# A hybrid decoder trunk on one core: window copies, side work, keys and values of layer B, planner durations, state rows, recurrent weights and tile sizes changed together

## The chip, the cores and the metric

The kernel runs on one core of one Trainium2 chip. The metric is the device time of one execution in microseconds; the median of several runs is compared. TensorE is called PE, VectorE DVE, ScalarE ACT, GpSimd POOL and SyncE SP, as in the profile.

## The reference

Four layers in a row, A, B, C and A again, for a prompt of 1024 tokens and 8 sequences of 4 sample tokens that share the weights; model width 1024, all float32. After each layer stands a LayerNorm of `ALPHA * x + mixer(x)`.

```python
def short_conv_mixer(x, buf, w_in, conv_w, w_out):            # layer A, twice
    h, b_gate, c_gate, z = jnp.split(x @ w_in, 4, axis=-1)
    conv, new_buf = causal_dwconv(c_gate * h, buf, conv_w)
    return (jax.nn.silu(z) * b_gate * conv) @ w_out, new_buf

def nsa_mixer(x, past_rows, win_buf, w_in, w_cmp, w_out):     # layer B
    proj = x @ w_in                                           # q, six kinds of k and v, gates, z
    full = jnp.concatenate([past_rows, rows], axis=1)
    kv_c = jnp.einsum('bnjcgd,cjgd->bncgd', blocks, w_cmp)    # 32 rows into one
    # attention over compressed blocks, 16 selected blocks and a window of 512
    y = (o * jax.nn.silu(z)) @ w_out
    all_win = jnp.concatenate([win_buf, win_new], axis=1)
    return y, rows, all_win[:, all_win.shape[1] - keep:]

def rglru_mixer(x, h0, buf, w_in, conv_w, conv_b, w_a, b_a, w_x, b_x, lam, w_out):   # layer C
    u, z = jnp.split(x @ w_in, 2, axis=-1)
    uc, new_buf = causal_dwconv(u, buf, conv_w)
    r, i = sigmoid(block_dense(uc, w_a) + b_a), sigmoid(block_dense(uc, w_x) + b_x)
    a = jnp.exp(-RG_C * softplus(-lam) * r)
    h = scan(a, sqrt(1 - a * a) * i * uc)                     # h[t] = a[t] h[t-1] + b[t]
    return (jax.nn.silu(z) * h) @ w_out, h[:, -1], new_buf
```

Besides the activations the outputs hold the new states: the last rows ahead of each convolution, the last `h`, the new rows of keys and values, and for the 8 sample sequences the window cache `nsa_win_sample`. Its 512 rows of 256 numbers are the old rows 4 to 511, moved up by four, and four new rows. The 508 old rows of a sequence are 520,192 bytes that are only copied.

## The kernel before

All 1056 tokens go together, in three token pieces j of 352 columns, and in 8 chunks c of 128 channels. Activations lie with the channels on the partitions. Every float32 operand is split into a high and a low part, so that the product of one chunk and one piece with a 1024-wide weight is 24 matmuls of 128x128 by 128x352: 8 chunks of the contraction, three products each.

Instructions are not issued at once but recorded (`Rec`, line 241; therefore nearly all rows of the profile name the helper's line L310). At the end of a `part()` the planner `Rec.lay` (line 378) simulates the recorded steps with assumed durations and so fixes the order of PE, ACT, DVE and POOL; for a DMA from SP it assumes 100 ns of issue and 360 bytes per ns on a shared bus. The order of SP's DMAs comes from a scheduler behind it. Tiles come from rings: `w` (3 weight blocks, split), `ws` (4 or 5 staging tiles), `big` (18 tiles of 2112 columns), `c` (8 or 9 tiles of 512 columns), and in PSUM 5 banks `mm` and 3 banks `aux`. A tile can only be written when its last reader is through.

Three parts are recorded, with the attention over the prompt, ordered by a table of its own (`Plan`), between the second and the third:

- The first: the load of x, `layer_a(0)` (line 947), `out_phase` 0 (line 685) with its norm, and the projection of layer B (`b_project`, line 1375). Beside layer A0 goes `compress` (line 1271), which gathers 64 batches of 1 MB of the paged cache by indirect DMA from POOL, writes half of each on as raw rows (`raw<-big`) and reduces the other half on DVE and POOL. `share` (line 610) lets it go on by RATE = 0.7 batches with each of the 96 products of layer A0. At its end the sums go out to `kcd`.
- The second: `decode` (line 1622), the attention of the sample tokens: scores in 36 units, and the selection of blocks (`decode_select`) at units SELT = (3, 9, 18), which reads `sel<-kcd`.
- The third: `out_phase` 1 behind layer B, `layer_c` (line 1078), `out_phase` 2, `layer_a(1)`, called A1 here, and `final_phase` (line 814).

`out_phase` takes the pairs (c, j) in order: a dense product over all eight U (outputs of the mixer), added to x, the sums for the norm; `d = y - k` goes to a scratch tensor `dd` in DRAM, and the norm of a piece j reads it back (`c<-dd`), normalises it and splits it into the x tiles that the next layer's matmuls read. `put_rows` (line 935) transposes the state rows SC, which each chunk of a layer fills, with eight PE transposes (`aux<-idf,SC`) and writes them out; layers A and C end with it. In layer B the products for keys and values (`mm<-x,w` or `mm<-big,x`, 128x384) are taken for nine row tiles in groups of four, copied by ACT to tiles `c`, and `put_k` writes the keys, with the low half of one group to a scratch tensor `kl`. Layer C loads each weight when its chunk comes (`load_w`, `weights`). Layer C also issues the eight copies of the old window rows, DRAM to DRAM; they wait for nothing that holds them, and SP's order has them in the first part, beside layer A0.

Of the kernel before, what the change touches and what calls it, by code (L numbers as in the profile page):

```python
# [18 lines left out]
P = 128  # L19
# [221 lines left out]
class Rec:  # L241
# [136 lines left out]
    def lay(self):  # L378
# [45 lines left out]
        while True:  # L424
# [23 lines left out]
            if e == "SP":  # L448
                free[e] = s + 100
                bus = max(bus, s + 100) + o.size / 360  # L450
                o.end = bus + 2000
            else:
                free[e] = o.end = s + cost
                if o.size:
                    bus = max(bus, o.end) + o.size / 360
                    o.end = bus + 2000
# [42 lines left out]
class Trunk:  # L499
    def __init__(self, ctx, tc, io):  # L500
        self.ctx, self.tc, self.nc, self.io = ctx, tc, tc.nc, io
        self.rec = Rec(tc)
# [31 lines left out]
    def work(self, stack, nws, ncc):  # L534

        self.nwork = getattr(self, "nwork", 0) + 1
        self.nws = nws
# [22 lines left out]
    def ct(self, w=512, dt=F32):  # L560
        return self.cc.tile([P, 512], dt, name="c")[:, 0:w]
# [123 lines left out]
    def out_phase(self, pm, wsrc, U, X, ln, lp, res=None, done={}, spill=None, final=None, nxt=()):  # L685
# [81 lines left out]
        for c, j in order:  # L767
            if c not in W:
                take(c)
# [44 lines left out]
    def final_phase(self, pm, wsrc, U, X, ln, lp):  # L814
# [77 lines left out]
        def squares(j, n, c0, c1):  # L892
# [4 lines left out]
            for i in range(3):  # L897
                x = half(j, c0 // 4, i)[:, c0 % 4 * P:(c1 - 1) % 4 * P + P]
                nc.scalar.activation(self.ct((c1 - c0) * P), x, AF.Square, bias=nk[:, i:i + 1], accum_out=sq[:, j, i, n:n + 1])

        running = []
        for c, j in [(c, j) for c in range(4) for j in range(3)] + [(c, j) for j in range(3) for c in range(4, NCH)]:
            if c not in W:
                take(c)
# [42 lines left out]
    def layer_a(self, pm, a, X, lp, side=None, nxt=()):  # L947
# [3 lines left out]
        U = [None] * NCH  # L951
        SC = lp.tile([P, NCH, 36 if self.later else 18], F32, name="SC")
# [14 lines left out]
        for c in range(NCH):  # L967
# [6 lines left out]
            def step(w, j):  # L974
# [19 lines left out]
                else:  # L994
# [11 lines left out]
                    for a0, b0, v in parts:  # L1006
# [4 lines left out]
                        self.split(uh, ul, v, "act", "dve")  # L1011
            U[c] = self.view2(self.big(F32R))
# [10 lines left out]
        self.put_rows(pm, SC, 18, [(0, 2, io["o_conv_a_prompt"][a, 0]), (2, 18, io["o_conv_a_sample"][a].rearrange("b t f -> (b t) f"))])  # L1023
# [54 lines left out]
    def layer_c(self, pm, X, lp):  # L1078
# [7 lines left out]
        def conv_in(c, js):  # L1086

            if c not in UC:
                W = self.get_w(("c", c), lambda: self.load_w(win[:, c * P:(c + 1) * P], ("c", c)))
# [42 lines left out]
        def gates(c):  # L1132
            n, i = c // 2, c % 2
            if i == 0:
                WA[n] = weights(n)
# [47 lines left out]
        def gate_out(c):  # L1183
            h2, i = H[c // 2], c % 2
            W = self.load_w(win[:, D + c * P:D + (c + 1) * P], ("z", c))
            u = self.view2(self.big(F32R))
            U[c] = u
            for j in range(3):
# [7 lines left out]
                self.split(u[:, 0, sl], u[:, 1, sl], th, "act", "pool")  # L1196

            nc.sync.dma_start(win_s[c, 0:508, :], cache[c, 4:512, :], rk=[("z", c)])
        UC, GT, WA, H = {}, {}, {}, {}
        win_s = io["o_nsa_win_sample"][0].rearrange("b t c g d -> b t (c g d)")  # L1200
        cache = io["cache_nsa_win"][0].rearrange("b t c g d -> b t (c g d)")
# [1221 lines left out]
```

## Time and profile before

| what | value |
|---|---|
| median of three runs | 2428.99 us (2427.99 to 2431.45) |
| the profiled execution | 2425.75 us, span 2423.7 us |
| busy: PE, DVE, ACT, POOL | 2305.6, 1583.6, 1203.7, 959.3 us |
| granted clock, mean | 0.977 |

The stages, in us from the span's start: load of x to 35; layer A0 to 414, `out_phase` 0 from 430 to 534, norm and layer B's first keys and values to 600, the rest of the projection to 690, decode to 880, the prompt's attention to about 1475, `out_phase` 1 and its norm to 1600, layer C to 1832, `out_phase` 2 to 1926, layer A1 to 2302, `final_phase` to the end; the last matmul ends at 2407.85.

How the views are read. The windows table gives for a stretch (start:end) its length, then the busy time of PE, PE's weight loads, DVE, ACT and POOL with the number of instructions of each, the granted clock of PE (1.00 is 2.4 GHz, 0.50 is 1.2 GHz), the mean busy share of the 16 DMA engines, and the GB/s that they moved. A row of a timeline begins with start and length; the bracket at its end holds the time for which the engine had been idle and what released it. In the chain of waits each piece is what the next one waited for. PE does 24 matmuls of 128x352 in 3.9 to 4.0 us where nothing holds it up.

### The profile page before, as it was taken

What the parts mean: (1) busy time and instruction counts of PE and PEld (TensorE: products, weight loads), DVE (VectorE), ACT (ScalarE), POOL (GpSimd) and SP (SyncE); (2) the same over time, 40 slices, a digit from 0 to 9 for tenths busy, and PEclk for the clock granted to TensorE, in tenths of its full rate; (3) what the DMA queues carried; (4) which work ended last, traced back from release to release, by engine and by line L of the source; (5) the groups of instructions that cost most, each with busy time, mean ns of one, the idle gap of its engine ahead of it and who ended that gap; (6) DMA issues with size and microseconds to landing.
All of it is one profiled execution on the core that took longest, in us unless ns stands there. A gap on an engine that the chain in (4) does not pass through costs nothing. (4 is left out here: it accounts for less than half of the span.)

```text
span 2423.7 us, 41400 instructions
## 1 busy us (share of the span) xinstructions
PE 2305.6 (95%) x14801; PEld 2234.8 (92%) x14801; DVE 1583.6 (65%) x3686; ACT 1203.7 (50%) x2757; POOL 959.3 (40%) x1070
## 2 busy tenths in 40 slices
PE   8999997997989989999999999989999999999996
PEld 8999997996888879999999989989999999999996
DVE  5786875575358877777777777787765753433336
ACT  3211111234438878888888883487863442222233
POOL 3454543213137765565555552333463320000131
PEclk9999999997999999999999999999999999999998
DMA  7999988347356752111111234331113321111112
GB/s 260 351 350 338 321 291 281 98 151 245 104 175 230 247 201 56 33 47 43 47 48 41 78 123 124 117 103 53 53 47 118 99 67 53 44 44 53 35 46 72
DMA packets 334642, 320.34 MB, mean 132 GB/s; under 512 B 19462, under 2 KB 301542, under 8 KB 324964
## 3 DMA queue, kind: packets, MB, share of 16 engines
q1 hardware_dynamic: 325220, 250.58, 33.4%
q0 software_dynamic: 9216, 67.11, 7.4%
q8 instruction: 117, 1.92, 0.3%
q14 instruction: 89, 0.73, 0.1%
HBM read 237.31 MB, written 84.48 MB: 133 GB/s over the span
## 5 line engine op out<-in xcount | busy, mean ns | idle before, releaser
L310 PE MATMUL mm<-x,w 128*128 128x352 f32 x5760 | 948.9, 326 | 29.6 <-DVE ws L310 10.3
L310 PEld LDWEIGHTS mm<-x,w 128*128 128x128 f32 x5760 | 936.4, 190 | 36.6 <-DVE w L310 7.6
L310 PE MATMUL mm<-big,w 128*128 128x352 f32 x2208 | 375.4, 325 | 1.0 <-ACT c L310 1.0
L310 PEld LDWEIGHTS mm<-big,w 128*128 128x128 f32 x2208 | 357.2, 189 | 2.8 <-ACT c L310 1.3
L310 POOL TENSOR_TENSOR w<-ws,w 128x1024 fp32r<-128x1024 f32 (+1 forms) x43 | 104.8, 2438 | 445.8 <-ACT w L310 426.7
L1968 DVE TENSOR_TENSOR c<-T,c 128x512 fp32r<-128x512 f32 (+1 forms) x320 | 204.7, 648 | 49.3 <-ACT c L1964 44.9
L1964 ACT CAST c<-T 128x512 fp32r<-128x512 f32 (+1 forms) x320 | 174.3, 551 | 59.3 <-PE T L1960 37.7
L310 ACT CAST w<-ws 128x1024 fp32r<-128x1024 f32 (+2 forms) x116 | 120.3, 1038 | 163.3 <-PE mm L310 119.4
L641 PE MATMUL D<-x,w 128*128 128x352 f32 x1008 | 195.5, 330 | 2.2 <-DVE big L2095 2.2
L1870 PE MATMUL A<-big 128*128 128x320 f32 (+11 forms) x832 | 181.5, 334 | 3.4 <-DVE ast L1895 1.6
L1975 PE MATMUL O<-c,big 128*128 128x256 f32 x1056 | 180.4, 291 | 0.5 <-ACT c L1964 0.2
L310 POOL TENSOR_TENSOR big<-big,ws 128x1024 f32<-128x1024 f32 (+1 forms) x38 | 89.6, 2358 | 199.0 <-DMA big<-in_cache_nsa_kv,idx 103.9
L641 PEld LDWEIGHTS D<-x,w 128*128 128x128 f32 x1008 | 159.8, 188 | 5.7 <-DVE big L2095 3.5
L310 DVE TENSOR_TENSOR big<-big 128x256 f32<-128x256 f32 (+3 forms) x204 | 150.5, 758 | 21.7 <-POOL big L310 20.3
L310 DVE TENSOR_TENSOR w<-ws,w 128x1024 fp32r<-128x1024 f32 (+2 forms) x73 | 93.9, 1286 | 105.6 <-ACT w L310 104.8
L310 ACT CAST big<-aux 128x352 fp32r<-128x352 f32 (+3 forms) x116 | 45.4, 399 | 229.9 <-DVE aux L310 160.6
L1975 PEld LDWEIGHTS O<-c,big 128*128 128x128 f32 x1056 | 147.2, 189 | 2.5 <-DVE c L1968 0.7
L1928 POOL TENSOR_SCALAR pr<-pr,G,ast 128x32 f32<-128x32 f32 (+6 forms) x192 | 125.6, 668 | 47.1 <-DVE ast L1939 41.3
L1870 PEld LDWEIGHTS A<-big 128*128 128x128 f32 x832 | 134.3, 193 | 10.0 <-PE A L1870 2.2
L310 ACT ACTIVATE aux<-ws,PT 128x352 f32<-128x352 f32 (+2 forms) x72 | 42.7, 593 | 172.5 <-DVE ws L310 167.9
L1924 ACT ACTIVATE pr<-pr,ast 128x32 f32<-128x32 f32 (+6 forms) x192 | 118.4, 619 | 18.3 <-DVE ast L1895 17.4
L310 DVE SCALAR_TENSOR_TENSOR c<-c,mm 128x352 f32<-128x352 f32 x125 | 64.1, 515 | 92.3 <-ACT c L310 54.6
(286 smaller groups left out, 4032.7 us busy)
## 6 DMA issues: line engine op xcount, KB each, us to landing
ws<-in_a_w_in SPq DMA_DIRECT2D x64, 512.0 KB
raw<-big SPq DMA_DIRECT2D x128, 256.0 KB
big<-raw SPq DMA_DIRECT2D x128, 256.0 KB
c<-dd SPq DMA_DIRECT2D x48, 176.0 KB
xs<-x SPq DMA_DIRECT2D x24, 352.0 KB
x<-xs SPq DMA_DIRECT2D x8, 1056.0 KB
ws<-in_a_w_out SPq DMA_DIRECT2D x16, 512.0 KB
ws<-in_c_w_in SPq DMA_DIRECT2D x16, 512.0 KB
```

What stands on the lines that cost most here:

```text
L310: getattr(real, name)(*[f(x) for x in a], **{q: f(x) for q, x in k.items()})
L641: self.nc.tensor.matmul(ps, a, b, start=n == 0, stop=n == 23 and last)
L1870: nc.tensor.matmul(o, q[:, hl, i * P:(i + 1) * P], k, start=m == 0, stop=m == 1)
L1924: nc.scalar.activation(S[:, a:a + m], S[:, a:a + m], AF.Exp, bias=st[:, k:k + 1], scale=-1.0, accum_out=st[:, 3 + k:4 + k])
L1928: nc.gpsimd.tensor_scalar(S[:, a:a + m], S[:, a:a + m], G[:, i, 16 * k + h:16 * k + h + 1], st[:, 6 + k:7 + k], op0=ALU.mult, op1=ALU.mult)
L1964: nc.scalar.copy(x["H"][:, 0:n], x["tp"][:, 0:n])
L1968: nc.vector.tensor_sub(x["L"][:, 0:n], x["tp"][:, 0:n], x["H"][:, 0:n].bitcast(F32))
L1975: nc.tensor.matmul(O, v, M[:, y * P:(y + 2) * P], start=done[0] == 0, stop=done[0] == total - 1)
```

## The change

- **Window copies.** The eight DRAM-to-DRAM copies of layer C are gone. In layer A1 (the call without side work) chunk c = 0 to 3 takes a `big` tile and loads two sequences into it, each as 127 partitions of four rows (127x1024); chunk c + 1 writes them out.
- **Side work.** RATE goes from 0.7 to 0.75.
- **Planner.** A DMA from SP is now assumed to take 400 ns of issue, the bus 330 bytes per ns.
- **State rows.** Layers A and C no longer call `put_rows` at their end but leave the call in `self.rows`; `out_phase` and `final_phase` make it ahead of the pair (2, 0).
- **Layer B.** `put_k` takes the second group first; the keys and values of four row tiles share one `big` tile, `four`, in place of four `c` tiles.
- **Selection.** SELT becomes (5, 10, 18).
- **Layer C's weights.** `take` and `fetch` load a block one ahead of its use in ORDER_C.
- **Small tiles.** In the third part the ring `c` has 12 tiles of 384 columns, not 9 of 512; the squares of `final_phase` are written to an `aux` bank in PSUM.

```diff
@@ -448,4 +448,4 @@
             if e == "SP":
-                free[e] = s + 100
-                bus = max(bus, s + 100) + o.size / 360
+                free[e] = s + 400
+                bus = max(bus, s + 400) + o.size / 330
                 o.end = bus + 2000
@@ -454,3 +454,3 @@
                 if o.size:
-                    bus = max(bus, o.end) + o.size / 360
+                    bus = max(bus, o.end) + o.size / 330
                     o.end = bus + 2000
@@ -501,3 +501,3 @@
         self.ctx, self.tc, self.nc, self.io = ctx, tc, tc.nc, io
-        self.rec = Rec(tc)
+        self.rec, self.rows = Rec(tc), None
 
@@ -533,6 +533,6 @@
 
-    def work(self, stack, nws, ncc):
+    def work(self, stack, nws, ncc, cw=512):
 
         self.nwork = getattr(self, "nwork", 0) + 1
-        self.nws = nws
+        self.nws, self.cw = nws, cw
         self.ws = Ring(self.rec, self.pool(f"ws{self.nwork}", nws, stack), "ws", nws) if nws else None
@@ -559,4 +559,4 @@
 
-    def ct(self, w=512, dt=F32):
-        return self.cc.tile([P, 512], dt, name="c")[:, 0:w]
+    def ct(self, w, dt=F32):
+        return self.cc.tile([P, self.cw], dt, name="c")[:, 0:w]
 
@@ -767,2 +767,5 @@
         for c, j in order:
+            if (c, j) == (2, 0) and self.rows:
+                self.rows()
+                self.rows = None
             if c not in W:
@@ -898,3 +901,3 @@
                 x = half(j, c0 // 4, i)[:, c0 % 4 * P:(c1 - 1) % 4 * P + P]
-                nc.scalar.activation(self.ct((c1 - c0) * P), x, AF.Square, bias=nk[:, i:i + 1], accum_out=sq[:, j, i, n:n + 1])
+                nc.scalar.activation(self.aux(pm)[:, 0:(c1 - c0) * P], x, AF.Square, bias=nk[:, i:i + 1], accum_out=sq[:, j, i, n:n + 1])
 
@@ -902,2 +905,4 @@
         for c, j in [(c, j) for c in range(4) for j in range(3)] + [(c, j) for j in range(3) for c in range(4, NCH)]:
+            if (c, j) == (2, 0):
+                self.rows()
             if c not in W:
@@ -951,2 +956,3 @@
         U = [None] * NCH
+        win_s, win_c = (io[x][0].rearrange("b t c g d -> b t (c g d)") for x in ("o_nsa_win_sample", "cache_nsa_win"))
         SC = lp.tile([P, NCH, 36 if self.later else 18], F32, name="SC")
@@ -1011,2 +1017,11 @@
                         self.split(uh, ul, v, "act", "dve")
+            if side is None and c < 5:
+
+                if c:
+                    for i in range(2):
+                        nc.sync.dma_start(win_s[2 * c - 2 + i, 0:508, :].rearrange("(p t) f -> p t f", t=4), keep[:, i])
+                if c < 4:
+                    keep = self.big()[0:127, 0:2048].rearrange("p (b t f) -> p b t f", b=2, t=4)
+                    for i in range(2):
+                        nc.sync.dma_start(keep[:, i], win_c[2 * c + i, 4:512, :].rearrange("(p t) f -> p t f", t=4))
             U[c] = self.view2(self.big(F32R))
@@ -1022,3 +1037,4 @@
             pass
-        self.put_rows(pm, SC, 18, [(0, 2, io["o_conv_a_prompt"][a, 0]), (2, 18, io["o_conv_a_sample"][a].rearrange("b t f -> (b t) f"))])
+        self.rows = lambda: self.put_rows(pm, SC, 18, [(0, 2, io["o_conv_a_prompt"][a, 0]),
+                                                       (2, 18, io["o_conv_a_sample"][a].rearrange("b t f -> (b t) f"))])
         return U
@@ -1088,3 +1104,3 @@
             if c not in UC:
-                W = self.get_w(("c", c), lambda: self.load_w(win[:, c * P:(c + 1) * P], ("c", c)))
+                W = take(("c", c))
                 g = self.wsl(1083)
@@ -1134,3 +1150,3 @@
             if i == 0:
-                WA[n] = weights(n)
+                WA[n] = take(("g", n))
                 H[n] = self.big()[:, 0:2 * T].rearrange("p (a n) -> p a n", a=2)
@@ -1184,3 +1200,3 @@
             h2, i = H[c // 2], c % 2
-            W = self.load_w(win[:, D + c * P:D + (c + 1) * P], ("z", c))
+            W = take(("z", c))
             u = self.view2(self.big(F32R))
@@ -1196,7 +1212,22 @@
                 self.split(u[:, 0, sl], u[:, 1, sl], th, "act", "pool")
-
-            nc.sync.dma_start(win_s[c, 0:508, :], cache[c, 4:512, :], rk=[("z", c)])
         UC, GT, WA, H = {}, {}, {}, {}
-        win_s = io["o_nsa_win_sample"][0].rearrange("b t c g d -> b t (c g d)")
-        cache = io["cache_nsa_win"][0].rearrange("b t c g d -> b t (c g d)")
+        todo = []
+        for x in ORDER_C.split():
+            c = int(x[1])
+            key = ({"u": "c"}.get(x[0], x[0]), c // 2 if x[0] == "g" else c)
+            if key not in todo:
+                todo.append(key)
+
+        def fetch(key):
+            w, c = key
+            if key not in self.pre:
+                self.pre[key] = weights(c) if w == "g" else self.load_w(win[:, (w == "z") * D + c * P:(w == "z") * D + (c + 1) * P], key)
+
+        def take(key):
+
+            fetch(key)
+            i = todo.index(key)
+            for k in todo[i + 1:i + 2]:
+                fetch(k)
+            return self.pre.pop(key)
         for x in ORDER_C.split():
@@ -1207,4 +1238,4 @@
                 (gates if x[0] == "g" else gate_out)(c)
-        self.put_rows(pm, SC, 36, [(0, 3, io["o_lru_conv_prompt"][0, 0]), (3, 27, io["o_lru_conv_sample"][0].rearrange("b t f -> (b t) f")),
-                                   (27, 28, io["o_lru_h_prompt"][0]), (28, 36, io["o_lru_h_sample"][0])])
+        self.rows = lambda: self.put_rows(pm, SC, 36, [(0, 3, io["o_lru_conv_prompt"][0, 0]), (3, 27, io["o_lru_conv_sample"][0].rearrange("b t f -> (b t) f")),
+                                                       (27, 28, io["o_lru_h_prompt"][0]), (28, 36, io["o_lru_h_sample"][0])])
         return U
@@ -1403,3 +1434,3 @@
 
-            for g in range(2):
+            for g in (1, 0):
                 kd = K[br]
@@ -1429,2 +1460,3 @@
                 kn = []
+                four = self.big()
                 if half == 1 and g4 == 0:
@@ -1442,3 +1474,3 @@
                     next(side, None)
-                    kv = self.ct(nw)
+                    kv = four[:, len(kn) * nw:(len(kn) + 1) * nw]
                     if half == 0:
@@ -2208,3 +2240,3 @@
 OUTS = ((0, 0), (0, 1), (1, 0), (1, 1))
-RATE = 0.7
+RATE = 0.75
 GAHEAD = 3
@@ -2229,3 +2261,3 @@
 SEL0 = 1
-SELT = (3, 9, 18)
+SELT = (5, 10, 18)
 DSH = dict(sel=7.1, kin=-11.8, begin=-11.6, keys=2.2, score=-10.9, turn=30.4, pv=-26.1, vin=-88.9, first=-37.1, vals=-23.0,
@@ -2371,3 +2403,3 @@
         lp = k.small(c1)
-        k.work(c1, 5, 9)
+        k.work(c1, 5, 12, 384)
         pm = banks(c1, "pm_1")
```

What this does to the order is shown at three places. The first is PE at the end of layer A0. `mm<-x,w` are A0's products, `aux<-idf,SC` the transposes of the state rows, `mm<-big,w` the products of `out_phase`, whose `big` are the U tiles. Before:

```order
L310 MATMUL mm<-x,w 128x352 x2226
L310 MATMUL aux<-idf,SC 18x128 x8
L310 MATMUL mm<-big,w 128x352 x36
L310 MATMUL aux<-c,ones_m 128x352
L310 MATMUL mm<-big,w 128x352 x24
L310 MATMUL aux<-c,ones_m 128x352
L310 MATMUL mm<-big,w 128x352 x24
```

After:

```order
L310 MATMUL mm<-x,w 128x352 x2226
L310 MATMUL mm<-big,w 128x352 x120
L310 MATMUL aux<-c,ones_m 128x352 x2
L310 MATMUL mm<-big,w 128x352 x6
L310 MATMUL aux<-c,ones_m 128x352
L310 MATMUL mm<-ws,ones_m 128x352 x2
L310 MATMUL mm<-big,w 128x352 x18
L310 MATMUL mm<-ws,ones_m 128x352
L310 MATMUL aux<-idf,SC 18x128 x8
L310 MATMUL mm<-big,w 128x352 x24
```

The transposes stood between A0's last product and the first of `out_phase`; now 168 matmuls of `out_phase` and some of its sums stand ahead of them. The count of DVE's compress steps (`big<-big`, `big<-big,ws`) behind its copy of the last chunk's SC goes from 14 to 24, by DVE's order.

The second is SP around the copies, from the end of the norm of `out_phase` 2 into layer A1. `ws<-in_a_w_in` are A1's weights, `c<-dd` what the norm reads back. Before:

```order
L310 DMA c<-xc 128x352
L310 DMA c<-dd 128x352
L310 DMA c<-xc 128x352
L310 DMA c<-dd 128x352 x5
L310 DMA ws<-in_a_w_in 128x8x128 x28
L310 DMA ws<-in_a_w_out 128x8x128 x5
```

After:

```order
L310 DMA c<-xc 128x352
L310 DMA dd<-c 128x352
L310 DMA big<-in_cache_nsa_win 127x1024 x2
L310 DMA ws<-in_a_w_in 128x8x128
L310 DMA out_nsa_win_sample<-big 127x1024 x2
L310 DMA ws<-in_a_w_in 128x8x128
L310 DMA big<-in_cache_nsa_win 127x1024 x2
L310 DMA out_nsa_win_sample<-big 127x1024 x2
L310 DMA c<-dd 128x352 x5
L310 DMA ws<-in_a_w_in 128x8x128 x6
L310 DMA big<-in_cache_nsa_win 127x1024 x2
L310 DMA out_nsa_win_sample<-big 127x1024 x2
```

Five `c<-dd` that followed other reads of the norm directly now stand behind four loads and four stores of window rows; a further two loads and two stores stand behind six of the weights, and the last (not in the piece) behind four more. Each store waits for the landing of its load. In before the copies stand in SP's first 75 rows as `out_nsa_win_sample<-in_cache_nsa_win 16x8128`.

The third is ACT at the first keys and values of layer B. `big<-ws` is the first half of a weight's split, `COPY` from `mm` empties a bank of keys and values, `c<-c,PT` and `x<-c` are the norm. Before:

```order
L310 ACTIVATE c<-c,PT 128x352
L310 CAST x<-c 128x352
L310 ACTIVATE c<-c,PT 128x352 x2
L310 CAST x<-c 128x352 x2
L310 CAST big<-ws 128x1024
L310 COPY c<-mm 128x384
L310 ACTIVATE c<-c,PT 128x352
L310 COPY c<-mm 128x384
```

After:

```order
L310 CAST big<-ws 128x1024
L310 CAST x<-c 128x352 x2
L310 ACTIVATE c<-c,PT 128x352 x2
L310 CAST x<-c 128x352
L310 COPY big<-mm 128x384 x4
L310 CAST x<-c 128x352
L310 ACTIVATE c<-c,PT 128x352 x2
L310 CAST x<-c 128x352 x2
L310 CAST big<-ws 128x1024
```

Four of the copies now stand ahead of the last weight's cast; before, the first of them stood behind it. On PE the matmuls of this stage ahead of the first `aux<-c,eb` go from 126 to 162. On SP the first `sel<-kcd` stood behind fourteen `big<-raw`, loads of decode's raw rows, with the last `kl` and one of these directly ahead of it; now it stands behind seven, with the last `kl` and three of them directly ahead.

## Rows read from the trace of the kernel before

**Rows 1.** Page: busy time of the engines; queue of SP (packets, MB, share).

```profile
PE 2305.6 (95%) x14801; PEld 2234.8 (92%) x14801; DVE 1583.6 (65%) x3686; ACT 1203.7 (50%) x2757; POOL 959.3 (40%) x1070
...
q1 hardware_dynamic: 325220, 250.58, 33.4%
```

**Rows 2.** Windows table, core 0; columns as in the section on the profile.

```profile
35.00:225.00 190.00, 188.99 (x1172) 188.14 (x1172) 141.81 (x224) 35.94 (x63) 96.72 (x57) 1.00 0.99 337
225.00:430.00 205.00, 176.63 (x1065) 173.70 (x1066) 143.27 (x238) 36.27 (x67) 94.15 (x53) 0.96 0.92 299
534.00:600.00 66.00, 47.21 (x221) 41.48 (x220) 39.70 (x71) 32.22 (x61) 24.04 (x23) 0.79 0.80 270
...
1930.00:2302.00 372.00, 369.61 (x2298) 368.86 (x2297) 150.44 (x294) 94.17 (x169) 32.16 (x26) 1.00 0.18 50
```

**Rows 3.** Timeline of PE, end of layer A0: start, length, instruction, [idle before <-releaser].

```profile
426.22 1.02 PE L310 MATMUL aux<-idf,SC 128*18 128x128 f32 x4 [12.33 <-DVE big L310]
429.06 1.02 PE L310 MATMUL aux<-idf,SC 128*18 128x128 f32 x4 [1.82 <-DVE big L310]
```

**Rows 4.** Timeline of DVE there, and the waits of DVE, 225 to 430.

```profile
419.45 1.52 DVE L310 TENSOR_TENSOR big<-big,ws 128x1024 f32<-128x1024 f32 x1 [4.82 <-DMA big<-in_cache_nsa_kv,idx]
...
DVE big L310 <- DMA big<-in_cache_nsa_kv,idx: 13.0, 5, 4.8
```

**Rows 5.** Windows table around the gap.

```profile
420.00:430.00 10.00, 1.96 (x9) 1.11 (x10) 7.36 (x16) 0.90 (x2) 2.34 (x1) 0.50 0.61 196
430.00:435.00 5.00, 5.00 (x27) 5.00 (x27) 1.89 (x7) 1.56 (x3) 0.00 (x0) 0.80 0.39 146
```

**Rows 6.** Layer A1: the chain of waits (start, length, what).

```profile
1924.78 5.06 DMA c<-xc
...
1946.91 354.78 PE mm L310 x2208
```

**Rows 7.** The eight copies of before, by tile; transfers of 35 to 320 us.

```profile
L310 SPq DMA_DIRECT2D out_nsa_win_sample<-in_cache_nsa_win x8: 534/694/1307, 25.2 to 226.0; - x8
...
DMA packets 87935, 94.59 MB, mean 332 GB/s; under 512 B 2958, under 2 KB 81654, under 8 KB 81654
```

**Rows 8.** Timelines of ACT and of PE at layer B.

```profile
578.63 1.04 ACT L310 CAST big<-ws 128x1024 fp32r<-128x1024 f32 x1 [2.58 <-DMA ws<-in_b_w_in]
579.58 0.47 ACT L310 COPY c<-mm 128x384 f32<-128x384 f32 x1
...
580.11 2.29 PE L310 MATMUL mm<-w,x 128*128 128x384 f32 x6 [8.67 <-ACT c L310]
```

**Rows 9.** Timelines of SP and of PE at the selection.

```profile
699.48 0.32 SPq L310 DMA_DIRECT2D sel<-kcd  x1
...
702.98 0.66 PE L310 MATMUL aux<-idf,sel 128*128 128x128 f32 x2 [7.35 <-DMA sel<-kcd]
```

**Rows 10.** Waits of PE, 1475 to 1760: total us, times, longest.

```profile
PE mm L310 <- ACT w L310: 3.9, 2, 2.7
PE mm L310 <- DVE w L310: 3.6, 4, 2.3
```

**Rows 11.** Timelines of ACT and of PE in the last phase.

```profile
2389.77 0.60 ACT L310 ACTIVATE c<-big,fstat 128x384 f32<-128x384 f32 x1
...
2404.78 0.73 PE L310 MATMUL aux<-idf,c 128*128 128x128 f32 x3 [2.34 <-DVE c L310]
2406.98 0.87 PE L310 MATMUL aux<-idf,c 128*128 128x128 f32 x3 [1.47 <-ACT ws L310]
```

**Rows 12.** Layer A1: timelines of SP and PE; GB/s in 40 slices of 2335 to 2360.

```profile
1935.00 5.81 SPq L310 DMA_DIRECT2D c<-dd  x5
...
1946.69 18.60 PE L310 MATMUL mm<-x,w 128*128 128x352 f32 x114
...
GB/s 0 0 0 0 0 0 0 0 0 0 0 0 0 89 207 296 406 397 406 387 302 26 0 13 0 0 0 0 0 0 26 0 0 0 0 0 0 13 0 0
```

## The prediction

> **What bounds the kernel now.** I read the page first: TensorE (PE) is busy 2305.6 of 2423.7 us [rows 1], so what a new order can win is the 118 us in which PE stands, plus the matmuls that run below full clock. The stage windows [rows 2] show where these lie: 35 to 225 has PE busy 188.99 of 190, but 225–430, the rest of layer A0, leaves 28.4 us, and 534–600, the start of layer B, 18.8. The second column to read is DMA share: 0.99 and 0.92 in A0, so the side work `compress` goes there at the pace of the transfers; in layer A1 (1930–2302) it is 0.18 and PE is busy 369.6 of 372. Then come the single waits of PE, one by one. The attention's plan is not touched. Each term is set against the profiled run, 2425.75 us, 3.2 below the median 2428.99.
>
> **Part 1: end of layer A0 (side work, state rows, copies out of it).** PE's timeline [rows 3] shows waits of 12.33 and 1.82 us that end with DVE's `big`, ahead of `aux<-idf,SC`, the eight transposes of put_rows. PE runs what it has in the written order, so out_phase's first matmuls, most of whose U tiles are there, stand behind them. DVE did not work through that gap: it waited 4.82 us for a gathered batch, its longest of five such waits (13.0 us) [rows 4], and behind it stood the last splits of U. The chain is gather, compress step, U[7] and SC, transposes. The matmuls behind it pay again: the granted clock is 0.50 in 420–430 and 0.80 in 430–435 [rows 5], which is 1 us each.
> Removed: the transposes go behind unit (2,0) of out_phase. PE then has some 90 matmuls (five banks, 18 of 24 products each, before U[6] and U[7] are read) at 354.78/2208 = 0.161 us [rows 6], 14.5 us, to lay over a wait of 14.2. The eight DRAM-to-DRAM copies (4.16 MB, issued from 25 to 226 us) leave a stage that moves 332 GB/s [rows 7]: 4.16/0.332 = 12.5 us for which the gathers no longer queue. Either covers the gap; the other 14 us of idle in 225–430 come from the same lateness of DVE, and the planner's slower bus (330, SP 400) and RATE 0.75 place the compress steps among DVE's work nearer to when batches land. What may be late next is DVE again, with 24 instead of 14 vector steps of compress behind the copy of SC[7]. Between 12 (the long gap alone) and 30 (all idle and the clock) I take **−25**, nearer to the upper end, since one gap has two covers.
>
> **Part 2: layer B's keys and values.** At 580.11 PE ends a wait of 8.67 us for a PSUM bank that ACT's `COPY c<-mm`, begun at 579.58, empties [rows 8]. Ahead of that copy stood `CAST big<-ws`, which had waited 2.58 us for a weight's landing, and before it the norm's activations. In the new order four such copies come ahead of that cast, and PE has 162 matmuls, not 126, before it needs `eb`: 36 × 0.161 × 384/352 = 6.3 us. The keys' low halves go out one group earlier. The wait may also only move to the norm's x tiles. From 4 lost (one more wait like the stretch's smaller ones; half of 8.67) to 13 won (the wait and half-clock matmuls behind it, mean 0.79 in 534–600 [rows 2]): **−7**. `four` takes three buffers of the 18 for a time; they come free with their DMAs, and no wait of this stretch is for one: 0.
>
> **Part 3: selection's keys.** PE waits 7.35 us for `sel<-kcd` [rows 9], issued at 699.48. In SP's row it stood behind fourteen loads of raw rows and the last write `kl`; now it stands behind seven, and the turn of its user is at unit 5, not 3, so PE scores more units ahead of it: **−7**, 0 to −9.
>
> **Part 4: layer C's weights** are fetched one block ahead. PE's waits that end with `w` in 1475–1760 are 3.9 + 3.6 us [rows 10]: **−6**, 0 to −8. **Part 5: the last phase.** The squares (0.60 us each [rows 11]) write into PSUM; at −0.1 to +0.1 us each on an ACT that PE seldom waits for this is nothing. Of the two last gaps, 2.34 and 1.47 [rows 11], some goes because DVE has the last `c` ahead of its normalising: **−2**, +1 to −4. 12 × 384 tiles have the bytes of 9 × 512; three more buffers only relax waits. The deferred rows of layers C and A1 stand among matmuls that show no gap: 0 ± 3.
>
> **Part 6: the copies' new place.** Eight loads and eight stores of 127x1024 (520 kB each) now stand in layer A1, on SP. In bytes this is 8.3 MB in a stage of 372 us at 50 GB/s [rows 2]; near the end of the kernel two 128x1024 loads and a weight moved at 406 GB/s [rows 12], so it is 20 us of transfers in all, hidden. In SP's queue, behind the first two loads stand a weight, two stores that wait for those loads' landing, two more loads, two stores, and then **five `c<-dd`**, which feed the norm of token piece 2. Before, those went out from 1935.00, in 5.81 us, and PE reaches piece 2 after 144 matmuls of A1: 102 until 1946.69 and 42 × 0.161, near 1953.5 [rows 6, 12]. If the copies land as others do (a c<-xc took 5.06 us there from issue to the norm's use [rows 6]), two rounds of load and store take 4 × 3 to 4 × 5 us from about 1927.5; c<-dd leaves 5 to 10 us later, within the slack of 12.7: **0**, +6 at most.
> No large transfer in this trace has a row count that 16 does not divide, so the other bound is all 127 rows on one of the 16 DMA engines. One engine's share of 406 GB/s is 25.4 kB/us, 20.5 us a copy; by the run's queue row (250.58 MB in 33.4% of 16 × 2423.7 us [rows 1]) it is 19.3 kB/us, 26.9 us. That is the slower rival below; the end I take is the one nearest to the rows that there are, large loads over 128 partitions.
> The Trainium skill speaks against this part: "DMA: Bandwidth & Descriptors", section "Why a DMA increments its semaphore by 16 and not by 1", says that a DMA of SP runs on the largest number of engines up to 16 that divides the slowest dimension of both its sides, and gives 127 partitions as a case of one engine. No run shown here tests it; by it the rival holds, and without it the 0 above.
>
> **Sum**: 25 + 7 + 7 + 6 + 2 + 0 = 47; 2425.75 − 47 = 2379, and with 3.2 to the median **2382 us**. With the terms' bounds, of which not all fall on one side, the likeliest case runs from 2362 to 2408.
>
> **Rivals.**
> *One engine for each copy (slower).* The queue on that engine from 1927.5: loads 0 and 1 (41 us), stores (82), loads 2 and 3 (123), stores (164), and c<-dd's share behind them, landing near 2091.5 against 1953.5: PE stands 138 us. Then each of two further rounds holds SP and so A1's weights for 4 × 20.5 = 82 us, and PE has four to five blocks of 72 matmuls (11.6 us each) in hand, about 52: twice 30. Together 198, with half clock at the restarts 200: **2582 us**. With 26.9 us a copy 189 + 2 × 55: 2681; with one block more in hand each time and 10 us less in the first wait, 2549. It decides from 8.5 us a copy (two to three engines): 8 × 8.5 − 26 = 42 and the half clock behind it eat the whole gain. For it: no row contradicts it, and c<-dd stands right behind the copies. Against it: all large transfers of before land fast.
> *Half the gain is eaten by new waits.* DVE's compress steps behind SC[7] delay out_phase as they did the transposes, and B's wait moves to the x tiles: parts 1 and 2 give 12 and 0, the sum is 27 or less: **2402 to 2412**.
> *The order does not bring compress forward.* If its end is set by the gathers' turn-around (POOL, the ring) and not by bytes, 12.5 us are not won and the steps that the planner puts later hold U[7] by as much: parts 1 to 5 give 22, less 20 of new waits: **2424 to 2432**, no difference.
>
> **How the numbers follow.** Forecast 0.48, half eaten 0.14, no difference 0.03, one engine 0.32, a loss from elsewhere 0.03. A difference below 0.2% (4.9 us) can't be told from none. So faster 0.62, same 0.03, slower 0.35. The range must take in half of the slow case: 2362 to 2590 leaves out 0.05 below and some 0.15 above. The likeliest case alone: 2362 to 2408.
>
> **What will show it.** Right: no gap over 3 us ahead of `aux<-idf,SC` and out_phase begun before 418; no 8.67 and no 7.35 some 20 and 30 us earlier than now; the copies in A1 landing in 3 to 6 us with PE above 99% there. Wrong: landings of 20 us and more of the 127-row copies, a gap of PE that ends with a norm tile some 25 us into A1 and two later ones that end with `w`; or DVE waiting for gathers as long as before at the end of A0.

## The result and the profile after

The changed kernel takes 2585.52 us (median of four runs, 2582.7 to 2587.48), against 2428.61 us before: the ratio is 1.0643, with a 95% interval of 1.0624 to 1.0661. It is 157 us slower. The profiled execution has a span of 2585.7 us.

The page shows the same work of PE in a longer span, and where it stood. Busy time of the engines, then PE and its granted clock in 40 slices of 64.6 us:

```profile
PE 2304.9 (89%) x14801; PEld 2232.7 (86%) x14801; DVE 1591.0 (62%) x3686; ACT 1198.2 (46%) x2755; POOL 957.3 (37%) x1070
...
PE   9999998989999999999999999999952197499997
...
PEclk9999998999999999999999999999976598799998
```

PE's busy time hardly moved (2305.6 in [rows 1]). The slices from the thirtieth on (1875 to 2260 us) hold the loss, and the clock is down there, to its lower level of 1.2 GHz (0.50) where PE stands longest. The stages tell it in two windows: layer A1 and the rest of the kernel, with the window in which nothing ran (columns as before):

```profile
1893.70:2465.50 571.80, 383.81 (x2331) 381.43 (x2330) 153.91 (x299) 96.44 (x172) 37.06 (x30) 0.83 0.15 48
2465.50:2586.00 120.50, 101.71 (x657) 100.40 (x655) 61.34 (x135) 40.05 (x109) 26.95 (x20) 0.93 0.19 64
...
1960.00:2020.00 60.00, 0.00 (x0) 0.00 (x0) 0.00 (x0) 0.00 (x0) 0.00 (x0) 0.50 0.09 34
```

Layer A1 took 378 us before (1924 to 2302) and takes 571.8 now, 193.8 more, at almost the same number of matmuls; 8 us of that are matmuls at lower clock (383.81 us busy, against 375.6 in the same stretch of before). For 60 us in the middle no engine did anything, while the DMA engines were busy 0.09 of the time and moved 34 GB/s. Everything ahead of A1 and behind it together became 32 us shorter: A1 begins at 1893.71 and not at 1924.11.

The timeline of PE has four waits in A1 that matter:

```profile
1934.81 0.95 PE L310 MATMUL mm<-x,w 128*128 128x352 f32 x2 [30.96 <-ACT w L310]
...
2057.66 0.66 PE L310 MATMUL mm<-x,w 128*128 128x352 f32 x1 [103.33 <-ACT x L310]
...
2166.26 48.29 PE L310 MATMUL mm<-x,w 128*128 128x352 f32 x288 [15.95 <-ACT c L310]
2251.34 48.91 PE L310 MATMUL mm<-x,w 128*128 128x352 f32 x291 [36.80 <-ACT c L310]
```

Together 187.0 us. What SP did meanwhile is the answer to [rows 12]; start, length, what is issued:

```profile
1882.92 0.38 SPq L310 DMA_DIRECT2D ws<-in_a_w_in  x1
...
1890.38 8.67 SPq L310 DMA_DIRECT2D big<-in_cache_nsa_win  x2
1899.14 19.60 SPq L310 DMA_DIRECT2D ws<-in_a_w_in  x1
1918.83 21.16 SPq L310 DMA_DIRECT2D out_nsa_win_sample<-big  x2
1940.09 19.61 SPq L310 DMA_DIRECT2D ws<-in_a_w_in  x1
1959.74 21.06 SPq L310 DMA_DIRECT2D big<-in_cache_nsa_win  x2
1994.33 25.93 SPq L310 DMA_DIRECT2D out_nsa_win_sample<-big  x2
2020.36 23.80 SPq L310 DMA_DIRECT2D c<-dd  x5
```

A weight's DMA that takes 0.38 us to issue ahead of the copies is held behind them for 19.60 and 19.61 us, and the five `c<-dd` for 23.80 (5.81 in [rows 12]). The chain of waits names the transfers that PE's waits come from (start, length):

```profile
1899.14 34.49 DMA ws<-in_a_w_in
...
1969.72 44.33 DMA big<-in_cache_nsa_win
...
2020.36 33.59 DMA c<-dd
...
2213.19 34.50 DMA ws<-in_a_w_in
```

The weight issued at 1899.14 landed 34.49 us later, which is the wait of 30.96; the `c<-dd` at 2020.36 + 33.59 = 2053.95, which is the wait of 103.33. The fourth wait, 36.80, ends with the weight issued at 2213.19; the third, 15.95, ends when ACT, which had stood behind a late weight, empties a bank again at 2165.75. And the transfer rates in 40 slices of 2077 to 2130, when little else than two loads and then two stores of window rows were under way:

```profile
DMA  7992000000010000000000000001000000000000
GB/s 192 324 290 86 28 25 28 28 25 28 25 40 25 28 25 28 25 28 25 28 25 28 25 28 28 25 28 37 28 25 28 25 28 25 28 25 28 25 28 25
```

A level of 25 to 28 GB/s, in which the share of the DMA engines is below a tenth: one sixteenth of the 406 GB/s of [rows 12] is 25.4. SP's queue from 1985 to 2015, when a load and, from 1994 on, a store beside it were under way (packets, MB, share of the 16 engines), gives the share itself:

```profile
q1 hardware_dynamic: 195, 0.79, 6.4%
```

One engine of 16 is 6.25%. So load and store together ran on what amounts to one engine, at 26 GB/s. At 26.5 GB/s a copy of 520,192 bytes takes 19.6 us, the time for which SP was held.

The end of layer A0 answers to [rows 3, 4]. PE, then ACT and DVE:

```profile
406.25 5.95 PE L310 MATMUL mm<-big,w 128*128 128x352 f32 x36
...
434.87 1.51 PE L310 MATMUL mm<-big,w 128*128 128x352 f32 x3 [8.55 <-ACT big L310]
...
434.37 1.14 ACT L310 CAST big<-aux 128x352 fp32r<-128x352 f32 x3 [16.68 <-DMA raw<-big]
...
429.64 1.22 DVE L310 TENSOR_TENSOR big<-big,ws 128x1024 f32<-128x1024 f32 x1 [3.85 <-DMA big<-in_cache_nsa_kv,idx]
```

out_phase begins at 406.25 instead of 429.74, but stands 8.55 us later, when it needs the last U: ACT could not write it for 16.68 us, by its row for `raw<-big`, the writing on of a gathered batch from a `big` tile, and DVE's last wait for a batch ends at 429.64, 10 us later than before (419.45). PE does 144 matmuls of `out_phase` ahead of the transposes (the 120, 6 and 18 of its order; the 168 named with the change is too many).

### The profile page after: what moved, and what is told of

It reads as the page before. It is cut to its first block, busy times and chain, and to the rows that moved or that the text cites. A ratio compares the mean times of both kernels' runs of the same rounds, so it can differ in the third digit from the quotient of the medians.

```text
span 2585.7 us, 41371 instructions
## 1 busy us (share of the span) xinstructions
PE 2304.9 (89%) x14801; PEld 2232.7 (86%) x14801; DVE 1591.0 (62%) x3686; ACT 1198.2 (46%) x2755; POOL 957.3 (37%) x1070
## 5 line engine op out<-in xcount | busy, mean ns | idle before, releaser
L310 PE MATMUL mm<-big,w 128*128 128x352 f32 x2208 | 383.6, 329 | 16.6 <-ACT big L310 8.5
L310 DVE TENSOR_TENSOR big<-big 128x256 f32<-128x256 f32 (+3 forms) x204 | 172.2, 864 | 22.7 <-POOL big L310 20.7
L310 POOL TENSOR_TENSOR big<-big 128x512 fp32r<-128x512 f32 (+2 forms) x74 | 86.4, 1184 | 109.2 <-DVE big L310 83.2
L310 DVE TENSOR_TENSOR c<-c 128x352 f32<-128x352 f32 (+1 forms) x85 | 51.5, 634 | 110.6 <-DMA c<-dd 109.0
```

The lines of the kernel that those rows point to most:

```text
L310: getattr(real, name)(*[f(x) for x in a], **{q: f(x) for q, x in k.items()})
```

## Experiments

Each was compared with the kernel before on the same chip; a ratio below is that of those runs, and times of different groups of runs (e1 to e4, e5 to e8, e9 to e12, e13 and e14) are best compared by their ratios. Of two such ratios the difference is uncertain by about 0.003, some 7 us.

**The theory** after the result: 127 rows put a whole window transfer on one DMA engine (the slower rival of the prediction). **The rival**: it is the place, SP's queue with stores that wait for loads ahead of what PE needs, whatever the rows.

**e1: 64 rows instead of 127.**

```diff
-                        nc.sync.dma_start(win_s[2 * c - 2 + i, 0:508, :].rearrange("(p t) f -> p t f", t=4), keep[:, i])
+                        nc.sync.dma_start(win_s[2 * c - 2 + i, 0:508, :].rearrange("t f -> (t f)").rearrange("(p e) -> p e", p=64), keep[64 * i:64 * i + 64])
...
-                    keep = self.big()[0:127, 0:2048].rearrange("p (b t f) -> p b t f", b=2, t=4)
+                    keep = self.big()[:, 0:2032]
...
-                        nc.sync.dma_start(keep[:, i], win_c[2 * c + i, 4:512, :].rearrange("(p t) f -> p t f", t=4))
+                        nc.sync.dma_start(keep[64 * i:64 * i + 64], win_c[2 * c + i, 4:512, :].rearrange("t f -> (t f)").rearrange("(p e) -> p e", p=64))
```

> The changed kernel with one edit: each of the 16 window transfers in layer A1 is cut as 64 rows of 2032 numbers instead of 127 rows of 1024, the same 520,192 bytes through the same `big` tile at the same chunks. Theory one engine (127 rows put a whole transfer on one of the 16 DMA engines, 19.6 us each): each transfer now lands in 2 to 5 us, the waits of 31, 103 and 53 us of TensorE in layer A1 go, 2585 - 187 = 2398, so 2390 to 2402 us. Rival place (it is the queue: stores that wait for their loads stand ahead of five c<-dd and of the weights, whatever the rows): most of the 187 us stay, 2540 us or more.

Measured: 2387.4 us, ratio 0.9821 (0.98 to 0.9842). The same bytes at the same place cost PE almost nothing; SP's rows of that stretch and PE's waits from 1870 to 2300:

```profile
1889.08 1.39 SPq L310 DMA_DIRECT2D ws<-in_a_w_in  x1
1893.41 3.19 SPq L310 DMA_DIRECT2D out_nsa_win_sample<-big  x2
...
1899.54 3.41 SPq L310 DMA_DIRECT2D c<-dd  x5
...
PE aux L310 <- DVE c L310: 0.6, 1, 0.6
```

0.6 us of waits are left of 187. The queue's order is nearly that of the changed kernel (the five `c<-dd` come three transfers earlier), and stores still wait for loads: 28.3 us of waits of SP in A1, which cost PE nothing. So the place is not the cause; the 127-row form is the whole loss. e1 changes two things in the form, the number of rows (127 to 64) and their length (4096 to 8128 bytes); e4 below keeps the length.

**e3: the 127-row copies alone**, on the kernel before (the copies of layer C out, the change's block of layer A1 in).

> The kernel before with the copies moved to layer A1 as in the change, 127 rows each, and nothing else of it. Theory one engine: all of the loss is here, 2428 + 187 less what layer A0 wins (0 to 12), so 2600 to 2620 us, with landings of about 20 us. Rival (the loss needs the other edits too, by the planner's new durations that put c<-dd behind the copies): under 2520 us.

Measured: 2632.54 us (one run), 201 us over the kernel before on that chip (2431.34) and above the 2600 to 2620 that were expected. The other edits aren't needed for the loss. Against e2, which differs from it only in the form of the copies (64 rows, 2438.56 us), it is 194 us, what layer A1 lost in the changed kernel; the other 7 are those by which e2 is slower than the kernel before.

**e4: other row counts**, of the same length, 4096 bytes.

```diff
-                        nc.sync.dma_start(win_s[2 * c - 2 + i, 0:508, :].rearrange("(p t) f -> p t f", t=4), keep[:, i])
+                        n = (126, 125, 124, 122)[c - 1]
+                        nc.sync.dma_start(win_s[2 * c - 2 + i, 0:4 * n, :].rearrange("(p t) f -> p t f", t=4), keep[0:n, i])
...
+                    n = (126, 125, 124, 122)[c]
...
-                        nc.sync.dma_start(keep[:, i], win_c[2 * c + i, 4:512, :].rearrange("(p t) f -> p t f", t=4))
+                        nc.sync.dma_start(keep[0:n, i], win_c[2 * c + i, 4:4 + 4 * n, :].rearrange("(p t) f -> p t f", t=4))
```

> The changed kernel with the window transfers of 126, 125, 124 and 122 rows of 1024 for the first to the fourth pair of sequences; the last 4 to 20 of the 508 rows of each sequence are left out. Theory divisor (as many engines as the largest number up to 16 that divides the rows: 14, 5, 4 and 2): a single transfer at 26.5 kB per us and engine takes 1.4, 3.9, 4.8 and 9.4 us, so the later pairs show steps of that size, the first pair lands like any other, and the time is 2392 to 2430 us. Rival (every count that 16 does not divide goes to one engine): 19 us each, four pairs alike, and 2560 to 2590 us.

Measured: 2393.11 us (one run). The queue of SP tells the counts apart. These are its rows for three stretches of 8 us in which only window copies were under way: 1900 to 1908 (125 rows), 1952 to 1960 (124) and 2000 to 2008 (122):

```profile
q1 hardware_dynamic: 261, 1.03, 31.8%
...
q1 hardware_dynamic: 215, 0.85, 25.9%
...
q1 hardware_dynamic: 104, 0.42, 12.7%
```

That is 129, 106 and 52 GB/s, beside 26 for 127 rows: as 5 to 4 to 2 to 1. The shares say the same in sixteenths of the engines (5 are 31.25%, 4 are 25%, 2 are 12.5%). And 5, 4, 2 and 1 are the largest numbers up to 16 that divide 125, 124, 122 and 127. SP's waits for loads agree: its stores of 122 rows leave at 1998.25, 13.2 us after the loads began. So the rival (all such counts alike) falls. For 126 rows other transfers lie between; their loads, issued at 1887.30, had landed by 1894.6, when both their stores had left, and no level of their own can be read.

SP's order here is that of the changed kernel, transfer for transfer: the five `c<-dd` again follow the loads and stores of the first two pairs of sequences. PE's waits from 1870 to 2300 are 4.0 us. So the place costs at most 4 of the 187 us, without the shift of order that e1 has.

**e2 and e10: what is it worth to take the copies out of layer A0?** e2 is the kernel before with the 64-row copies in A1; e10 the changed kernel with the DRAM-to-DRAM copies put back into layer C and nothing in A1.

> The kernel before with one edit: the eight DRAM-to-DRAM copies are gone and the 16 transfers of 64 rows stand in layer A1. Theory bytes (the copies cost layer A0 12.5 us of transfers, and its end hangs on the transfers): the gap ahead of the state rows' transposes shortens by about as much, 2414 to 2420 us. Theory turn-around (the end of layer A0 hangs on when the gathers and their buffers take turns, not on bytes): 2424 to 2431 us, no difference.

Measured: 2438.56 us, ratio 1.0036 (1.0019 to 1.0054): slower, by 0.36%.

> The changed kernel with the eight DRAM-to-DRAM copies as before, in 16 rows each, and nothing in layer A1; all other edits stay. Theory bytes (taking 4.16 MB out of layer A0 is part of the gain): 12 us slower than with the 64-row copies, 2397 to 2401 us. Theory turn-around (layer A0 ends when the gathers' turns end, the bytes lie in between): 2384 to 2391 us, no difference.

Measured: 2375.02 us, ratio 0.9781 (0.9764 to 0.9799), where e1 has 0.9821: faster with the copies in layer A0. So both the bytes' theory and "no difference" fall. The trace agrees: without the copies the last gather is issued later, not earlier. Rows for the 64 gathers (durations, first and last start) of before, e2, e1 and e10:

```profile
L315 POOL DMA_INDIRECT big<-in_cache_nsa_kv,idx x64: 932/1021/2009, 37.1 to 416.6; - x64
...
L315 POOL DMA_INDIRECT big<-in_cache_nsa_kv,idx x64: 932/984/2014, 35.3 to 426.2; - x64
...
L315 POOL DMA_INDIRECT big<-in_cache_nsa_kv,idx x64: 933/979/2203, 34.7 to 426.7; - x64
...
L315 POOL DMA_INDIRECT big<-in_cache_nsa_kv,idx x64: 933/982/2199, 34.9 to 419.0; - x64
```

416.6 with them and 426.2 without on the kernel before, 419.0 and 426.7 on the changed one. The transfers of 35 to 330 us run at 334 GB/s in the kernel before and at 310 in e2, but up to 4.16 of the 7.2 MB between them are the copies themselves, which are gone. The gathers' own queue in that stretch, before and in e2 (packets, MB, share of the engines):

```profile
q0 software_dynamic: 7344, 53.48, 47.8%
...
q0 software_dynamic: 6997, 51.03, 48.1%
```

So the gathers got 2.45 MB less done by 330 us. Why the gathers get on better with the copies between is not settled: SP's order of the weights and the raw rows changes along with them, and no run took the two apart.

**e5, e6, e7: deferral or planner?** e5 is the kernel before with the deferred state rows alone; e6 the kernel before with the planner's durations alone (400 ns, 330); e7 is e1 with layer A0's state rows at its end again.

> The kernel before with the deferred state rows alone (layers A0, C and A1), all else as before. Theory of the prediction (the deferral uncovers 14 us of out_phase's work at the end of layer A0): the wait of 12.33 us goes, 2414 to 2418 us. Rival (the order of out_phase itself is what counts: with the old planner only 36 of its matmuls, 5.8 us, stand ahead of the first one that reads the last U, and the wait moves to it): the gap shrinks to 6 to 9 us, 2421 to 2427 us.

Measured: 2432.15 us, ratio 1.0013 (0.9993 to 1.0033), no difference that the runs can show, where both theories had expected a gain. The wait of 12.33 is now 1.05 + 8.49 + 2.08 inside out_phase.

> The kernel before with the planner's two durations alone (SP 400 ns, bus 330). By its order 90 matmuls of out_phase then stand ahead of the state rows' transposes, without any deferral. Theory planner (the gain at the end of layer A0 is the planner's): 14.5 us of work over the wait, 2410 to 2420 us. Rival deferral (the planner's durations only shift the side work): 2424 to 2432 us.

Measured: 2412.83 us, ratio 0.9921 (0.9899 to 0.9943).

> The kernel of 64-row copies (2387 us) with the state rows of layer A0 written out at its end again; the planner still lets 90 matmuls of out_phase pass ahead of them. Theory planner: 2386 to 2391 us, no difference. Theory deferral: the 12 to 14 us come back, 2399 to 2402 us.

Measured: 2388.7 us, ratio 0.9828 (0.9805 to 0.985), against 0.9821: no difference. The planner's two durations alone move 90 matmuls of out_phase ahead of the transposes; the deferral adds nothing visible to them and nothing without them. PE in e6, where the gap still stands behind these 90:

```profile
404.08 6.03 PE L310 MATMUL mm<-big,w 128*128 128x352 f32 x36 [0.77 <-DVE c L310]
...
433.71 1.02 PE L310 MATMUL aux<-idf,SC 128*18 128x128 f32 x4 [19.72 <-DVE big L310]
```

**e8, e9, e11: other parts, each taken out of e1.** e8 has layer B's keys and values in `c` tiles, the old group order and SELT (3, 9, 18); e9 loads layer C's weights at their use (without the two lines that fetch the next block); e11 has RATE 0.7.

> The kernel of 64-row copies (2387 us) with layer B's keys and values in single small tiles, the old order of the key groups and SELT (3, 9, 18). By the prediction's parts 2 and 3, 7 + 7 us: 2399 to 2403 us. Rival (the waits at layer B are those of the norm's tiles and hidden behind each other, only the selection counts): 2392 to 2396 us.

Measured: 2398.22 us, ratio 0.9868 (0.9845 to 0.9891): 0.0047 over e1's, 11 us. The three parts were taken out together. In the traces most of it stands at the selection: PE's wait for ACT at layer B is 7.3 us where e1 still has 5.5, but ahead of the first `aux<-idf,sel` PE waits 8.90 where e1 has no wait:

```profile
686.44 0.66 PE L310 MATMUL aux<-idf,sel 128*128 128x128 f32 x2 [8.90 <-DVE w L310]
```

> The kernel of 64-row copies (2387 us) with layer C's weights loaded at their use again, not one block ahead. By part 4 of the prediction the waits for w in layer C come back, 6 to 8 us: 2393 to 2396 us. Rival (these waits were covered by another): 2386 to 2390 us.

Measured: 2396.93 us, ratio 0.9871 (0.9853 to 0.9889): 12 us over e1's; by the intervals it may be 5 to 19, so 6 to 8 is not ruled out. In the traces the stretch from the attention to the end of `out_phase` 2 is 10.6 us longer than in e1 (839.77 to 1897.74, against 839.79 to 1887.17). The waits with `w` in 1440 to 1880 are back with 4.6 + 4.4 us, and two of together 3.2 for `x` beside them:

```profile
PE mm L310 <- DVE w L310: 4.6, 4, 2.7
PE mm L310 <- ACT w L310: 4.4, 2, 4.1
PE mm L310 <- ACT x L310: 3.2, 2, 2.1
```

> The kernel of 64-row copies (2387 us) with RATE 0.7. If the rate sets when the side work ends: 4 to 8 us slower, 2391 to 2396 us. If the transfers and the ring set it: 2385 to 2390 us.

Measured: 2385.04 us, ratio 0.9819 (0.98 to 0.9838): no difference.

**e12, e13, e14: what holds the end of layer A0?** If not the bytes, then perhaps the turns of the batches: a gather waits until the sum of the third batch ahead is there. In e12 (on e1), e13 (on e10) and e14 (on the kernel before):

```diff
-GAHEAD = 3
+GAHEAD = 5
```

> The kernel of 64-row copies (2387 us) in which a gather waits for the sum of the fifth batch ahead of it instead of the third, so that more gathers are under way. Theory turn-around (the gathers of layer A0 are held by the batches' turns): the wait of 10.25 us in out_phase shrinks, 2376 to 2384 us. Theory bytes (the transfers are at their limit): 2385 to 2391 us.

Measured: 2369.47 us, ratio 0.9763 (0.9744 to 0.9782), 0.0058 or 14 us under e1's. PE's wait of 10.25 us in out_phase is 1.05:

```profile
434.82 7.59 PE L310 MATMUL mm<-big,w 128*128 128x352 f32 x27 [10.25 <-ACT big L310]
...
418.94 3.07 PE L310 MATMUL mm<-big,w 128*128 128x352 f32 x15 [1.05 <-ACT big L310]
```

> The changed kernel with the eight DRAM-to-DRAM copies as before and five gathers ahead. If the copies and the gathers' turns are two separate levers on the end of layer A0 (2375 with the copies in layer A0, 2387 without; 2369 with five gathers ahead): 2355 to 2360 us. If both act on the same wait, the turn of the batches: 2366 to 2372 us, as with five gathers alone.

Measured: 2367.76 us, ratio 0.9738 (0.9713 to 0.9762), against 0.9763 for e12 and 0.9781 for e10. The ratios alone do not decide: two separate levers would give 0.9821 − 0.0040 − 0.0058 = 0.9723, which the interval still holds, and one lever the 0.9763 of e12. The traces speak for one: the last six matmuls of `out_phase` 0 begin at 525.07 in e1, at 516.20 with the copies back (e10), at 506.62 with five gathers ahead (e12) and at 503.96 with both (e13), so the copies that were worth 8.9 us are worth 2.7 beside the other. That is one trace of each. e13 has the lowest time of this study, not clearly apart from e12: the changed kernel with the copies left where they were and five gathers ahead, 61 us under the kernel before.

> The kernel before with five gathers ahead and nothing else. Theory turn-around (layer A0 of the kernel before ends when the turns of the batches end): the wait of 12.33 us and part of the 13.0 us of DVE's waits for gathers go, 2412 to 2422 us. Theory bytes (part 1 of the prediction): 2424 to 2432 us, no difference.

Measured: 2429.03 us, ratio 0.9997 (0.9979 to 1.0016): no difference. In the kernel before the last gather is not earlier for it (420.9 against 416.6), and PE waits 8.49 us for DVE's `ws` in A0 and 7.19 ahead of the second four transposes. So more gathers under way help the changed order and not the old one, where the wait only moves. That is as far as the runs go: which of the planner's moves makes the difference was not tried.

## Why the prediction was wrong

The forecast was 2382 us and faster; 2585.5 came out. The number is that of the prediction's slower rival, 2582, and inside the range, which had been drawn up to 2590 for it; the choice between the two was wrong, and with it the direction.

- **The step that failed is part 6, the choice of the 0.** It set the copies' cost to that of "the rows that there are, large loads over 128 partitions". But every one of those rows has a count that 16 divides; they could not speak on 127, so nearness to them was no reason. e1 and e4 show what stands in its place: the row count decides (it was the same on both sides of every copy here), and 127 rows run at a sixteenth of the rate, 19.6 us a copy. The Trainium skill's "DMA: Bandwidth & Descriptors", section "Why a DMA increments its semaphore by 16 and not by 1", which names 127 partitions as one engine, was right; the trace agrees, with 26 GB/s for 127 rows, 129 for the five engines of 125, 106 for the four of 124 and 52 for the two of 122.
- **The rival's own working held.** 138 us of the first wait: measured 30.96 + 103.33 = 134.3. Two further waits of 30: 15.95 + 36.80 = 52.8. Half clock at the restarts 2: about 8 in the whole stage. Sum 200, measured 193.8 in A1. That the total came within 4 us of 2582 is in part luck, since the 2382 under it was made of terms that were off both ways (below). Its count of 102 matmuls ahead of 1946.69 should be 96 (PE's rows before: 50 + 4 + 36 + 6), which moves its 1953.5 by 1 us. What it had not foreseen is that the first part falls on a weight: SP itself was held in issuing it, behind the copies.
- **Part 1 (25 us) was mis-sized and wrongly founded.** The last six matmuls of out_phase 0 begin at 524.41 instead of 532.15: 7.7 us. The price of the copies' bytes, 12.5 us, was of the wrong sign (e2, e10), and the deferral is worth nothing that the runs show (e5, e7); the gain is the planner's (e6: 9 us there in its trace, 17 us in all by the medians). Its 90 matmuls came out (93 ahead of the new wait, 15 us). The rival "half the gain is eaten by new waits" described this: the wait came back 15 us of work later.
- **Parts 2 and 3 (7 + 7)** held as a sum, and not each for its reason. From the end of out_phase 0 to the attention the lead over the kernel before grows from 7.7 to 862.42 − 841.37 = 21.1 us, by 13.4. Of these, 11.4 are won up to the 144 `mm<-x,big` that follow the keys and values (614.60 before, 595.48 now), and 2.0 after that. But the planner's durations alone win 6.9 of the 11.4 (e6: 598.49), and lose them again by the attention (853.18). Part 2's wait did not go: 5.85 us of its 8.67 stand, for ACT, at 564.56. Part 3's did, 7.35 to 0.39, and e8 shows that without these edits the selection would eat the earlier arrival: it reaches the 144 matmuls with e1 (596.51 against 596.35) and the attention 10.3 us later.
- **Part 4 (6)** was low: the lead grows by 9.3 us from the attention (21.1) to the end of out_phase 2 (1920.12 − 1889.71 = 30.4), and e9 puts the lookahead at 12, with the spread named there. **Part 5 (2)** held within its bounds: the last phase takes 120.5 instead of 121.6.

The rows for the leads, of the kernel before and then of the changed one (the selection's row last):

```profile
532.15 1.21 PE L310 MATMUL mm<-big 128*128 128x352 f32 x6
...
614.60 23.30 PE L310 MATMUL mm<-x,big 128*128 128x352 f32 x144
...
862.42 1.09 PE L1870 MATMUL A<-big 128*128 128x160 f32 x4 [1.08 <-ACT us L2026]
...
1920.12 4.00 PE L310 MATMUL mm<-big 128*128 128x352 f32 x24
...
524.41 1.21 PE L310 MATMUL mm<-big 128*128 128x352 f32 x6
...
595.48 23.30 PE L310 MATMUL mm<-x,big 128*128 128x352 f32 x144
...
841.37 0.63 PE L1902 MATMUL A<-big 128*128 128x160 f32 x4 [1.08 <-ACT us L2058]
...
1889.71 4.00 PE L310 MATMUL mm<-big 128*128 128x352 f32 x24
...
680.82 0.41 PE L310 MATMUL aux<-idf,sel 128*128 128x128 f32 x2 [0.39 <-DMA sel<-kcd]
```

With a working form of the copies the change gains 1.8% (e1), close to the 2382 of the forecast. That nearness is partly luck: part 1 was some 18 us too large, and the other parts some 10 too small.

## What to carry to other kernels

Before a transfer is given a new shape, look at the outermost count of both its sides: in these runs it set how many of the 16 DMA engines' worth of rate the transfer got, and 127 got one. The same bytes cut as 64 rows cost nothing. A missing row is not a cheap one: where no row of the trace has the new operation's property, the nearest row is no evidence, and a rival that no row contradicts deserves more weight than the forecast gave it. Bytes taken out of a busy stage need not be worth their transfer time; look for the wait at the stage's end and try that itself, here the number of gathers under way, before pricing bytes.

## What was unexpected of the hardware

SP did not run ahead of such a transfer: while two 127-row copies were under way, the issue of one ordinary weight DMA took 19.60 us instead of 0.38, so that everything behind it in SP's order was late too, even transfers that nothing else held. Why the issue itself is held, no run shows. And layer A0's gathers got on more slowly without the eight large copies (51.03 against 53.48 MB by 330 us, e2 and before), with the last of them some 10 us later; the cause is open.
